# The first norm moved behind the first product, and gate biases and sinks loaded as one row

## Chip, core and metric

The kernel runs on one core of a Trainium2 chip. The metric is the device time of one execution in microseconds (us); lower is better. Engines are named as in the profile: PE is the matrix engine (PEld its weight loads), DVE the vector engine, ACT the scalar engine, POOL the GpSimd engine, SP the engine whose queue issues most DMAs.

## Reference

Two decoder layers of width 1024 over 256 tokens, float32. Only the start matters here: a norm of each token, then a product with `w_in`, whose column groups feed the mixers.

```python
def rmsnorm(x, g):
    xf = x.astype(jnp.float32)
    y = xf * lax.rsqrt(jnp.mean(xf * xf, axis=-1, keepdims=True) + EPS)
    return (y * g.astype(jnp.float32)).astype(x.dtype)
...
def mixer_block(h, w_in, conv_w, conv_b, b_igate, b_fgate, mlstm_norm_g, sinks,
                rel_bias, w_branch_m, w_branch_a, w_out):
    proj = h @ w_in
    mqk, mv, mo, mi, mf, aq, ak, av, ga, gb = jnp.split(proj, offsets, axis=-1)
...
for l in range(DEPTH):
    h = rmsnorm(x, norm_mix_g[l])
    x = x + mixer_block(h, w_in[l], conv_w[l], conv_b[l], b_igate[l], b_fgate[l], ...)
    h = rmsnorm(x, norm_mlp_g[l])
    x = x + sqrelu_mlp(h, w_up[l], w_down[l])
```

The norm of a token is one number per row, `r = rsqrt(mean(x*x) + EPS)`, so `(x * r * g) @ w` equals `r * ((x * g) @ w)`: the factor may be applied to the rows of the product.

## The kernel before

Tokens lie in two tiles of 128 (`tt` 0 and 1), the width of 1024 in eight blocks of 128 (`k` 0 to 7) and in two halves of 512 (`hf`). Every product is made in three passes: each operand is split into a rounded part (`hi`, `xh`) and the rest (`lo`, `xl`), and hi by hi, lo by hi and hi by lo are summed in PSUM (L220 to L222 with tokens as the stationary side, "xs"; L234 to L236 with weights as the stationary side, "ws").

Weights come in pieces of 128 x 1024 (512 KB). `pump_dma` (L114) issues the load of the next piece on SP into one of four buffers `raw`; `pump_hi` (L142) casts it to `hi` on ACT (L152); `pump_lo` (L123) subtracts on DVE (L127), which frees the raw buffer, and issues the next load. `hi` and `lo` have seven buffers each.

The order of all work is written by hand. `slots` is a list of steps, each 12 or 24 matmuls; `run_slots` (L191) emits for each slot first what is registered with `at`, then splits of pieces, then `at_late`, then `at_last`, then the matmuls of the slot, then what is registered with `after`. Each engine executes its own instructions in the order in which they were emitted, and waits where one needs a result of another engine. So an instruction that waits keeps back everything emitted later on its engine.

At the start, `setup_start` (L400) issues the loads of x (X, 128 x 2 x 1024) and of the first four pieces, then `small_loads` (L388): eleven small loads, of which six spread a few numbers to 128 partitions (`gb_bias`, `sink`). PE is kept busy with matmuls of a zero tile (`N_WARM`, L418, L424, L559).

`first_norm` (L524) squares X on ACT and DVE, takes the power -0.5 on POOL (`Norm.rstd`, L349), scales X by it (L532), transposes the 128 x 128 blocks on PE (L537) and multiplies by g while it splits into xh (ACT, L541) and xl (DVE, L547).

The first product, `mv` (columns 1024 to 2047 of `w_in`), has slots `s_mv` to `s_mv` + 7. Its first four slots take the two token tiles one after the other (head "t"): tile 0 on pieces 0 to 3, then tile 1 on them; the last four take piece by piece (tail "k"). `mv_evac` (L597) copies the four PSUM banks of it to `vm` behind slot `s_mv` + 7, two on ACT (L603) and two on DVE (L601). The next product, `kv` (four slots from `s_kv` = `s_mv` + 8, pieces 8 to 11), takes three of those banks again, so its first matmuls wait for these copies.

Beside `mv` run `setup_small` (L426, at slot `s_mv` + 2; masks and selectors on POOL) and `setup_cols` (L439, at slot `s_mv` + 4): two transposes on PE, the copies `cw` and `rbT` on DVE, then on POOL the table `Et` of the relative bias (a memset, 17 copies of a column of `rbT`, L450 and L455, and a DMA to DRAM, L457).

Of the kernel before, what the change touches and what calls it, by code (L numbers as in the profile page):

```python
# [17 lines left out]
P = 128  # L18
# [24 lines left out]
def trunk(ctx: ExitStack, tc: tile.TileContext, x, norm_mix_g, w_in, conv_w, conv_b, b_igate, b_fgate,  # L43
# [43 lines left out]
    def piece(w, kt, c0):  # L87
        def load(raw):
            nc.sync.dma_start(raw[:, :1024], w[kt * P : (kt + 1) * P, c0 : c0 + 1024])

        pieces.append((load, 1024))
        return len(pieces) - 1
# [21 lines left out]
    def pump_dma():  # L114
        j = n_dma[0]
        if j < len(pieces):
            raws[j] = wp.tile([P, 1040], F32, tag="raw", bufs=N_RAW, name=nm("raw"))
            pieces[j][0](raws[j])
            n_dma[0] += 1
# [3 lines left out]
    def pump_lo():  # L123
        for j in los:
            raw, n = raws.pop(j), pieces[j][1]
            hi, lo = pc[j]
            nc.vector.tensor_tensor(lo[:, :n], raw[:, :n], hi[:, :n].bitcast(F32), op=ALU.subtract)  # L127
            pump_dma()
        los.clear()

# [255 lines left out]
    N_WARM = (26, 16, 8)  # L386

    def small_loads():  # L388
        S0["b8"] = big8()
        rows = S0["rows"] = S0["b8"][:80, 0, 0:P]  # L390
        rb = S0["rb"] = const.tile([NB_BUCKETS, 16], F32, name="rb")
        nc.sync.dma_start(rb, rel_bias)
        for l in range(DEPTH):
            nc.sync.dma_start(gb_bias[:, l, 0:4], b_igate[l].partition_broadcast(P))
            nc.sync.dma_start(gb_bias[:, l, 4:8], b_fgate[l].partition_broadcast(P))
            nc.sync.dma_start(sink[:, l, :], attn_sinks[l].partition_broadcast(P))
            nc.sync.dma_start(rows[40 * l : 40 * l + 32, :], conv_w[l].rearrange("j (m c) -> (j m) c", c=P))
            nc.sync.dma_start(rows[40 * l + 32 : 40 * l + 40, :], conv_b[l].rearrange("(m c) -> m c", c=P))

    def setup_start():  # L400
        grow = big8()[:8, 0, 0:P]
        nc.sync.dma_start(X[:, 0, 0:512], xv[:, 0, 0:512])
        nc.sync.dma_start(X[:, 0, 512:], xv[:, 0, 512:])
        nc.sync.dma_start(grow, norm_mix_g[0].rearrange("(k c) -> k c", c=P))
        for i in range(N_RAW):
            if i == 3:
                nc.sync.dma_start(X[:, 1, :], xv[:, 1, :])
            pump_dma()
# [7 lines left out]
        pw = psA()  # L416
        for _ in range(N_WARM[0]):
            nc.tensor.matmul(pw[:, :P], mask, mask, start=True, stop=True)  # L418
        pg = psA()
        nc.tensor.transpose(pg[:, :8], grow, ident[:8, :8])  # L420
        S0["gcol"] = const.tile([P, KT], F32, name="gcol")
        S0["pg"], S0["pw"] = pg, pw
        for _ in range(N_WARM[1]):
            nc.tensor.matmul(pw[:, :P], mask, mask, start=True, stop=True)  # L424

    def setup_small():  # L426
        nc.vector.tensor_copy(identb, ident)
        nc.gpsimd.affine_select(
            out=mask, in_=mask, pattern=[[1, P]], compare_op=ALU.is_ge, fill=NEG, base=0, channel_multiplier=-1)
        nc.gpsimd.memset(vm[:, :, :, 256:257], 1.0)  # L430
        z = tmp()
        nc.gpsimd.memset(z, 0.0)
        nc.scalar.copy(Rs, z[:, 0:384])
        for r in (0, 32):
            nc.gpsimd.affine_select(out=z[r : r + 32, 0:4], in_=z[r : r + 32, 0:4], pattern=[[-1, 4]],
                                    compare_op=ALU.not_equal, fill=1.0, base=0, channel_multiplier=1)
        nc.scalar.copy(sel, z[:, 0:4])

    def setup_cols():  # L439
        pt = psB()  # L440
        nc.tensor.transpose(pt[:, :80], S0["rows"], ident[:80, :80])
        nc.vector.tensor_copy(cw, pt[:, :80])
        pt = psB()
        nc.tensor.transpose(pt[:16, :NB_BUCKETS], S0["rb"], ident[:NB_BUCKETS, :NB_BUCKETS])
        rbT = const.tile([16, NB_BUCKETS], F32, name="rbT")
        nc.vector.tensor_copy(rbT, pt[:16, :NB_BUCKETS])
# [77 lines left out]
    def first_norm(st, xtag, nxt):  # L524

        xh, xl = st["hT"] = xT_tiles(xtag)
        N = [Norm(0), Norm(1)]
        gcol, xn, pts = S0["gcol"], {}, {}

        def scale(tt, hf):  # L530
            xn[tt, hf] = tmp()
            nc.vector.tensor_scalar(xn[tt, hf], X[:, tt, hc(hf)], N[tt].r[:, :1], None, op0=ALU.mult)  # L532

        def tr(tt, hf):
            pts[tt, hf] = psB()
            for j in range(4):
                nc.tensor.transpose(pts[tt, hf][:, j * P : (j + 1) * P], xn[tt, hf][:, j * P : (j + 1) * P], ident)  # L537

        def hi(tt, ks):
            for k in ks:  # L540
                nc.scalar.activation(xh[:, k, tt * P : (tt + 1) * P], pts[tt, k // 4][:, k % 4 * P : (k % 4 + 1) * P],  # L541
                                     AF.Copy, scale=gcol[:, k : k + 1])

        def lo(tt, ks):
            for k in ks:
                s = slice(tt * P, (tt + 1) * P)
                nc.vector.scalar_tensor_tensor(xl[:, k, s], pts[tt, k // 4][:, k % 4 * P : (k % 4 + 1) * P],  # L547
                                               gcol[:, k : k + 1], xh[:, k, s].bitcast(F32), op0=ALU.mult,
                                               op1=ALU.subtract)

        N[0].square(0)
        N[0].square(1, "dve")
        N[0].rstd()
        nc.scalar.copy(gcol, S0["pg"][:, :8])
        pump_hi(0, 0)
        scale(0, 0)
        tr(0, 0)
        for _ in range(N_WARM[2]):
            nc.tensor.matmul(S0["pw"][:, :P], mask, mask, start=True, stop=True)  # L559
        pump_lo_part(0, 512)  # L560
        hi(0, (0, 1))
        lo(0, (0, 1))
# [3 lines left out]
        hi(0, (2, 3))  # L566
        pump_lo()
        lo(0, (2, 3))
        pump_hi(0, 2)
        N[1].square(0)  # L570
        N[1].square(1)
        pump_lo()
        N[1].rstd()
        scale(0, 1)
        pump_hi(0, 3)
        scale(1, 0)
        pump_lo()
        scale(1, 1)

        def tr_all(tt, hf):  # L580
            tr(tt, hf)
            hi(tt, range(4 * hf, 4 * hf + 4))
            lo(tt, range(4 * hf, 4 * hf + 4))

        for i in range(4):
            limits[nxt + i] = 3 + max(0, i - 1)
        slots[nxt + 1][0].insert(2, call(lambda: tr_all(1, 0)))
        slots[nxt + 2][0].insert(1, call(lambda: tr_all(0, 1)))
        slots[nxt + 2][0].insert(4, call(lambda: tr_all(1, 1)))


    def mixer(l, ta, tb):
        w = w_in[l]
        st = {}
        s_mv = xs_group(st, "mv", "hT", w, MV0, head="t")

        def mv_evac(tt, hf):  # L597
            o = vm[:, tt, 2 * hf : 2 * hf + 2, 0:256]
            i = st[("mv", tt, hf)].rearrange("p (h c) -> p h c", h=2)
            if hf:  # L600
# [145 lines left out]
        def cwc(j, m):  # L746
            return cw[:, 40 * l + j * 8 + m : 40 * l + j * 8 + m + 1]
# [318 lines left out]
    for l in range(DEPTH):  # L1066
# [9 lines left out]
        if l == 0:  # L1076
            at(s_mv + 2, setup_small)
# [84 lines left out]
```

## Time and profile before

| | us |
|---|---|
| median of 3 runs | 883.76 (883.75 to 883.88) |
| the profiled execution, its own time | 884.32 |
| its span in the profile | 882.5 |
| PE busy in the span | 868.5 (98%) |
| first matmul of the first product | at 9.21 |
| first matmul of kv | at 35.87 |
| last matmul | at 873.92 |

Times in the trace count from the start of the span; the 1.8 us between span and time lie around it. PE is busy almost throughout, so what counts is how late PE gets to a given matmul, and whether it is ever kept waiting after that. "Busy" of PE overstates in the first microseconds, since a matmul's end is modelled.

### The profile page before, as it was taken

The page shows a single profiled execution, that of the slowest core. Times are in us where ns is not written, and L with a number is a line of the kernel's source. Part 1 is how long each engine was busy: PE and PEld are TensorE (multiplying, and loading weights), DVE is VectorE, ACT ScalarE, POOL GpSimd, SP SyncE. Part 2 cuts the span into 40 slices and gives each one's busy share as a digit, 9 for nine tenths or more (in the row PEclk, how much of TensorE's full clock was granted, in tenths as well). Part 3 has the DMA queues.
Part 4 walks back from the last instruction along what each step waited for, and adds up shares of the span by engine and source line. Part 5 has one row for each costly group of instructions (what it writes and reads, how often), then busy time and mean ns, then how long its engine had stood idle before and what let it go on. Part 6 is the DMA issues. An engine that isn't in the chain of part 4 may idle for free.

```text
span 882.5 us, 15073 instructions
## 1 busy us (share of the span) xinstructions
PE 868.5 (98%) x5929; PEld 789.6 (89%) x5929; DVE 572.4 (65%) x928; ACT 468.2 (53%) x771; POOL 128.3 (15%) x164
## 2 busy tenths in 40 slices
PE   7999999999999999999999999999999999999996
PEld 5899889999989999998889997999998899999985
DVE  5758879666666654546574788876667764737363
ACT  5657776654355554544355557764634453636352
POOL 1360534120000000000002435322000000000000
PEclk9999999999999999999999999999999999999999
DMA  6875435445556747474655455354564466555621
GB/s 217 288 246 186 144 120 167 141 147 158 177 191 202 248 133 240 133 242 136 219 171 189 149 186 163 109 160 144 148 223 157 146 225 225 194 188 188 194 96 48
DMA packets 50711, 155.28 MB, mean 176 GB/s; under 512 B 7912, under 2 KB 10192, under 8 KB 50640
## 3 DMA queue, kind: packets, MB, share of 16 engines
q1 hardware_dynamic: 49456, 150.69, 52.8%
q0 software_dynamic: 896, 3.17, 1.0%
q8 instruction: 46, 0.75, 0.4%
q10 hardware_dynamic: 288, 0.46, 0.1%
q14 instruction: 25, 0.20, 0.1%
HBM read 153.23 MB, written 1.07 MB: 175 GB/s over the span
## 4 chain that ended last, share of the span: by engine, by line
PE 92%; DVE 3%; issue 2%; ACT 1%; POOL 1%; DMA 0%; POOLq 0%; SPq 0%; DVEq 0%; ACTq 0%
PE pa L220 13%; PE pa L221 13%; PE pa L222 12%; PE pa L235 10%; PE pa L234 10%; PE pa L236 10%; PE pb L235 5%; PE pb L234 5%; PE pb L236 5%; PE pb L859 1%; PE pb L322 1%; PE pb L879 1%; DVE lo L127 1%; PE pb L919 1%; PE pb L832 1%
## 5 line engine op out<-in xcount | busy, mean ns | idle before, releaser
L127 DVE TENSOR_TENSOR lo<-raw,hi 128x1024 fp32r<-128x1024 f32 (+1 forms) x276 | 332.0, 1226 | 137.5 <-ACT hi L152 134.4
L152 ACT CAST hi<-raw 128x1024 fp32r<-128x1024 f32 (+1 forms) x280 | 286.1, 1049 | 184.0 <-PE pa L222 48.1
L234 PE MATMUL pa<-xh,hi 128*128 128x256 f32 x864 | 246.4, 285 | 0.0
L235 PE MATMUL pa<-xl,hi 128*128 128x256 f32 x864 | 242.6, 281 | 0.0
L236 PE MATMUL pa<-xh,lo 128*128 128x256 f32 x864 | 241.7, 280 | 0.0
L234 PEld LDWEIGHTS pa<-xh,hi 128*128 128x128 f32 x864 | 162.7, 188 | 0.9 <-issue 0.3
L235 PEld LDWEIGHTS pa<-xl,hi 128*128 128x128 f32 x864 | 162.9, 189 | 0.3
L236 PEld LDWEIGHTS pa<-xh,lo 128*128 128x128 f32 x864 | 162.8, 188 | 0.0
L220 PE MATMUL pa<-hi,xh 128*128 128x512 f32 (+1 forms) x384 | 149.9, 390 | 1.8 <-ACT xh L541 1.8
L221 PE MATMUL pa<-lo,xh 128*128 128x512 f32 (+1 forms) x384 | 148.1, 386 | 0.5 <-DVE lo L127 0.4
L222 PE MATMUL pa<-hi,xl 128*128 128x512 f32 (+1 forms) x384 | 147.8, 385 | 0.0
L234 PE MATMUL pb<-xh,hi 128*128 128x256 f32 x384 | 107.6, 280 | 0.0
L235 PE MATMUL pb<-xl,hi 128*128 128x256 f32 x384 | 107.6, 280 | 0.0
L236 PE MATMUL pb<-xh,lo 128*128 128x256 f32 x384 | 107.3, 280 | 0.0
L220 PEld LDWEIGHTS pa<-hi,xh 128*128 128x128 f32 x384 | 72.2, 188 | 15.4 <-ACT xh L541 2.0
L222 PEld LDWEIGHTS pa<-hi,xl 128*128 128x128 f32 x384 | 72.1, 188 | 15.4
L221 PEld LDWEIGHTS pa<-lo,xh 128*128 128x128 f32 x384 | 72.2, 188 | 15.2 <-DVE lo L127 1.6
L349 POOL TENSOR_TENSOR sm<-sm,mhalf 128x1 f32<-128x1 f32 x9 | 6.6, 731 | 500.0 <-DVE sm L348 500.0
L235 PEld LDWEIGHTS pb<-xl,hi 128*128 128x128 f32 x384 | 72.3, 188 | 1.8
L234 PEld LDWEIGHTS pb<-xh,hi 128*128 128x128 f32 x384 | 72.2, 188 | 1.7
L236 PEld LDWEIGHTS pb<-xh,lo 128*128 128x128 f32 x384 | 72.3, 188 | 0.0
L220 PE MATMUL pa<-hi,b 128*128 128x512 f32 x124 | 48.8, 394 | 0.0
(210 smaller groups left out, 986.1 us busy)
## 6 DMA issues: line engine op xcount, KB each, us to landing
raw<-in_w_in SPq DMA_DIRECT2D x104, 512.0 KB, 4.5
raw<-in_w_up SPq DMA_DIRECT2D x64, 512.0 KB, 4.7
raw<-in_w_down SPq DMA_DIRECT2D x64, 512.0 KB, 4.3
raw<-in_w_branch_a SPq DMA_DIRECT2D x16, 512.0 KB, 3.5
raw<-in_w_branch_m SPq DMA_DIRECT2D x16, 512.0 KB, 4.1
raw<-in_w_out SPq DMA_DIRECT2D x16, 512.0 KB, 4.5
b<-ed SPq DMA_DIRECT2D x4, 512.0 KB, 5.2
g<-in_mlstm_norm_g POOLq DMA_DIRECT2D x2, 512.0 KB, 5.8
```

The source lines that it names most:

```text
L127: nc.vector.tensor_tensor(lo[:, :n], raw[:, :n], hi[:, :n].bitcast(F32), op=ALU.subtract)
L152: nc.scalar.copy(hi[:, :n], raw[:, :n])
L220: nc.tensor.matmul(b, xh[:, kt, s], wh[:, c], start=first, stop=False)
L221: nc.tensor.matmul(b, xh[:, kt, s], wl[:, c], start=False, stop=False)
L222: nc.tensor.matmul(b, xl[:, kt, s], wh[:, c], start=False, stop=last)
L234: nc.tensor.matmul(o, wh[:, c], xh[:, kt, :], start=first and half == 0, stop=False, skip_group_check=True)
L235: nc.tensor.matmul(o, wh[:, c], xl[:, kt, :], start=False, stop=False, skip_group_check=True)
L236: nc.tensor.matmul(o, wl[:, c], xh[:, kt, :], start=False, stop=last, skip_group_check=True)
L322: nc.tensor.transpose(pt[:, j * P : (j + 1) * P], src[:, j * P : (j + 1) * P], ident)
L832: nc.tensor.matmul(sp[:, P : 3 * P], q[:, P:T], kh[:, gk, :], start=False, stop=False, skip_group_check=True)
L859: nc.tensor.transpose(tp[:, j * P : (j + 1) * P], L[:, j * P : (j + 1) * P], ident)
L879: nc.tensor.matmul(o, va[:, 0, vs], PT[:, 0:T], start=(h0 % 4 == 0), stop=False, skip_group_check=True)
```

## The change

Four things change, all at the start of the first layer.

1. The first product takes x times g, without the norm. `first_norm` transposes X itself (L554), multiplies by g on DVE for a half tile at once into a float32 buffer `xg` (L560), and splits that (ACT L564, DVE L567) into `uh`, `ul`. The second halves of X follow inside slots `s_mv` + 2 and + 3 (`rest`). The squares and `rstd` of the two tiles (`norm`) come at the end of the preparations of slots `s_mv` + 3 and + 4. `mv_evac` multiplies by `r` of the token.
2. The other products of the layer still take the normed input. `rows` (at slot `s_mv` + 6) turns `r` into a row over tokens on all partitions with two matmuls (L613) and an ACT copy (L616); `normed` multiplies `xg` by it on DVE for four blocks at once (L621) and splits again (ACT L323, DVE L324), the first half at slot `s_mv` + 6, the second at + 7.
3. `mv` goes piece by piece from the start (head "k"), and piece 0 is loaded and split in two halves.
4. The small loads are six: both layers' convolution rows in two, and gate biases and sinks as one row of 48 numbers, which `setup_cols` spreads with a matmul (L459) and two DVE copies. `norm_mix_g` is loaded from ACT's queue. `setup_small` moves from slot `s_mv` + 2 to + 6, its two ACT copies to + 9.

```diff
+    def pump_hi_part(a, b):
+        j = n_split[0] - (1 if a else 0)
...
+        nc.scalar.copy(pc[j][0][:, a:b], raws[j][:, a:b])
...
-        for l in range(DEPTH):
-            nc.sync.dma_start(gb_bias[:, l, 0:4], b_igate[l].partition_broadcast(P))
-            nc.sync.dma_start(gb_bias[:, l, 4:8], b_fgate[l].partition_broadcast(P))
-            nc.sync.dma_start(sink[:, l, :], attn_sinks[l].partition_broadcast(P))
...
+        nc.sync.dma_start(rows[0:64, :], conv_w.rearrange("l j (m c) -> (l j m) c", c=P))
+        nc.sync.dma_start(rows[64:80, :], conv_b.rearrange("l (m c) -> (l m) c", c=P))
+        row = S0["row"] = S0["b8"][0:1, 0, 512:560]
...
+        nc.scalar.dma_start(grow, norm_mix_g[0].rearrange("(k c) -> k c", c=P))
+        for tt in range(2):
+            nc.sync.dma_start(X[:, tt, 0:512], xv[:, tt, 0:512])
+        pump_dma(2)
+        pump_dma()
+        pump_dma()
+        for tt in range(2):
+            nc.sync.dma_start(X[:, tt, 512:], xv[:, tt, 512:])
+        pump_dma()
         small_loads()
...
     def setup_cols():
...
+        nc.tensor.matmul(pt[:, :48], ones[0:1, 0:1].to_broadcast([1, P]), S0["row"], start=True, stop=True)
+        nc.vector.tensor_copy(gb_bias, pt[:, 0:16].rearrange("p (l c) -> p l c", l=DEPTH))
+        nc.vector.tensor_copy(sink, pt[:, 16:48].rearrange("p (l h) -> p l h", l=DEPTH))
...
+        def times_g(tt, hf):
+            nc.vector.tensor_tensor(xg[sl(tt, hf)], pts[tt, hf].rearrange("p (k t) -> p k t", k=4),
+                                    gcol[:, 4 * hf : 4 * hf + 4].unsqueeze(2).to_broadcast([P, 4, P]), op=ALU.mult)
...
+        def rest(tt):
+            tr(tt, 1)
+            times_g(tt, 1)
+            hi(tt, 1)
+            lo(tt, 1)
+
+        def norm(tt):
+            N[tt].square(0)
+            N[tt].square(1)
+            N[tt].rstd()
...
+        for tt in range(2):
+            slots[nxt + 2 + tt][0].insert(1, call(lambda tt=tt: rest(tt)))
+            at_last(nxt + 3 + tt, lambda tt=tt: norm(tt))
...
+        def rows():
+            pr = psB()
+            for tt in range(2):
+                nc.tensor.matmul(pr[:, tt * P : (tt + 1) * P], N[tt].r[:, 0:1].to_broadcast([P, P]), ident, start=True,
+                                 stop=True, skip_group_check=True)
+            S0["R"] = tmp()
+            nc.scalar.copy(S0["R"][:, 0:T], pr[:, 0:T])
+            st["hT"] = xT_tiles(xtag)
+
+        def normed(c):
+            s = (slice(None), slice(4 * c, 4 * c + 4), slice(None))
+            nc.vector.tensor_tensor(xg[s], xg[s], S0["R"][:, 0:T].unsqueeze(1).to_broadcast([P, 4, T]), op=ALU.mult)
+            evac_split(xg[s], st["hT"][0][s], st["hT"][1][s])
+
+        at(nxt + 6, rows)
+        at(nxt + 6, lambda: normed(0))
+        at(nxt + 7, lambda: normed(1))
...
-        s_mv = xs_group(st, "mv", "hT", w, MV0, head="t")
+        s_mv = xs_group(st, "mv", "hT" if l else "hU", w, MV0, head="t" if l else "k")
...
+            if l == 0:
+                r = S0["r"][tt]()
+                if hf:
+                    nc.vector.tensor_scalar(o, i, r, None, op0=ALU.mult)
+                else:
+                    nc.scalar.activation(o, i, AF.Copy, scale=r)
...
-            at(s_mv + 2, setup_small)
+            at(s_mv + 6, setup_small)
+            at(s_mv + 9, setup_copies)
             at(s_mv + 4, setup_cols)
```

Where this puts the instructions shows in three places. First POOL, at the powers of the norm: `sm<-sm,mhalf` is `rstd` of a token tile, `b<-rbT` are copies of the table, `ed` is its DMA to DRAM. Before:

```order
L349 TENSOR_TENSOR sm_174<-sm_173,mhalf 128x1
L349 TENSOR_TENSOR sm_225<-sm_224,mhalf 128x1
L428 AFFINE_SELECT mask<-mask 128x128
L430 MEMSET vm 128x8
L432 MEMSET tmp_286 128x512
L435 AFFINE_SELECT tmp_286<-tmp_286 32x4 x2
L448 MEMSET b_6_97 16x384
L450 COPY b_6_97<-rbT 16x16
L455 COPY b_6_97<-rbT 16x3
```

Now, from the last copies of the table on (the first tile's power stands ahead of the table's memset, as L359):

```order
L472 COPY b_6_99<-rbT 16x10 x2
L472 COPY b_6_99<-rbT 16x12
L472 COPY b_6_99<-rbT 16x14
L472 COPY b_6_99<-rbT 16x15
L474 DMA ed<-b_6_99 16x384
L359 TENSOR_TENSOR sm_358<-sm_357,mhalf 128x1
L436 AFFINE_SELECT mask<-mask 128x128
L438 MEMSET vm 128x8
```

The power of token tile 1 stood ahead of the whole table and now stands behind it.

Second PE, between the sixth and the seventh piece of the first product (`pa` are its banks; `pb<-ident,sm` are the two matmuls of `rows`). Before, at the end of the sixth piece (`hi_341`) and the start of the seventh:

```order
L220 MATMUL pa_243<-hi_341,xh_165 128x512
L221 MATMUL pa_243<-lo_342,xh_165 128x512
L222 MATMUL pa_243<-hi_341,xl_166 128x512
L220 MATMUL pa_240<-hi_389,xh_165 128x512
L221 MATMUL pa_240<-lo_390,xh_165 128x512
```

Now, at the end of the sixth (`hi_241`) and the start of the seventh:

```order
L230 MATMUL pa_201<-hi_241,xh_139 128x512
L231 MATMUL pa_201<-lo_242,xh_139 128x512
L232 MATMUL pa_201<-hi_241,xl_140 128x512
L613 MATMUL pb_406<-ident,sm_291 128x128
L613 MATMUL pb_406<-ident,sm_358 128x128
L230 MATMUL pa_198<-hi_244,xh_139 128x512
```

The two matmuls that need both powers stand in PE's order with 24 matmuls of the first product behind them.

Third DVE, from the copies of `setup_cols` to the evacuation of the first product (`lo<-raw,hi` is a piece's subtraction, `vm<-pa` the evacuation, `b_11` is `xg`, `tmp_409` the row of `r`). Before:

```order
L446 COPY rbT<-pb_363 16x32
L127 TENSOR_TENSOR lo_390<-raw_222,hi_389 128x1024
L127 TENSOR_TENSOR lo_393<-raw_236,hi_392 128x1024
L127 TENSOR_TENSOR lo_396<-raw_300,hi_395 128x1040
L127 TENSOR_TENSOR lo_422<-raw_345,hi_421 128x1040
L127 TENSOR_TENSOR lo_440<-raw_399,hi_439 128x1040
L127 TENSOR_TENSOR lo_458<-raw_403,hi_457 128x1040
L601 COPY vm<-pa_241 128x2x256
```

Now:

```order
L463 COPY rbT<-pb_317 16x32
L129 TENSOR_TENSOR lo_348<-raw_248,hi_347 128x1040
L358 TENSOR_SCALAR sm_357<-sm_143 128x1
L129 TENSOR_TENSOR lo_374<-raw_252,hi_373 128x1040
L435 CAST identb<-ident 128x128
L621 TENSOR_TENSOR b_11_141<-b_11_141,tmp_409 128x1024
L324 TENSOR_TENSOR xl_412<-b_11_141,xh_411 128x1024
L129 TENSOR_TENSOR lo_417<-raw_256,hi_416 128x1040
L621 TENSOR_TENSOR b_11_141<-b_11_141,tmp_409 128x1024
L324 TENSOR_TENSOR xl_412<-b_11_141,xh_411 128x1024
L129 TENSOR_TENSOR lo_438<-raw_283,hi_437 128x1040
L640 TENSOR_SCALAR vm<-pa_199,sm_291 128x2x256
```

The four wide instructions of `normed` now stand between the pieces' subtractions and ahead of the evacuation; on ACT the two casts of `normed` (L323) stand likewise ahead of its part of the evacuation (L642), each with the cast of a kv piece behind it.

More of the change, by code (lines that the diff above doesn't have):

```diff
@@ L384, in trunk @@
     S0 = {}
[L386 removed]
+    N_WARM = (22, 6, 14)
     def small_loads():
@@ L536, in tr @@
             for j in range(4):
[L537 to L559, printed above, removed]
+                c = hf * 512 + j * P
+                nc.tensor.transpose(pts[tt, hf][:, j * P : (j + 1) * P], X[:, tt, c : c + P], ident)
+        def sl(tt, hf):
+            return (slice(None), slice(4 * hf, 4 * hf + 4), slice(tt * P, (tt + 1) * P))
```

112 lines of the change are left out of this document (57 added, 55 removed).

## Prediction

> **What bounds the kernel now.** First the head of the page and its chain of waits (part 4): PE is busy 98% of the span, and 92% of the chain that ends last is PE.
>
> ```profile
> span 882.5 us, 15073 instructions
> PE 92%; DVE 3%; issue 2%; ACT 1%; POOL 1%; DMA 0%; POOLq 0%; SPq 0%; DVEq 0%; ACTq 0%
> ```
>
> Then busy time by stretches (first the stretch and its length, then PE's busy time in it).
>
> ```profile
> 36.00:60.00 24.00, 23.98 (x202) 23.77 (x201) 14.22 (x19) 12.15 (x16) 9.84 (x9) 1.00 0.75 241
> 60.00:100.00 40.00, 39.43 (x335) 38.46 (x335) 30.27 (x71) 27.99 (x55) 13.09 (x23) 1.00 0.60 199
> 100.00:200.00 100.00, 100.00 (x734) 91.03 (x734) 76.77 (x187) 65.27 (x147) 31.85 (x29) 1.00 0.47 144
> 200.00:400.00 200.00, 199.97 (x1345) 183.36 (x1345) 122.03 (x131) 95.21 (x115) 2.05 (x3) 1.00 0.58 192
> 400.00:600.00 200.00, 199.79 (x1351) 179.16 (x1350) 139.14 (x267) 115.91 (x220) 49.87 (x58) 1.00 0.52 163
> 600.00:872.00 272.00, 271.97 (x1791) 247.79 (x1790) 164.07 (x207) 127.76 (x172) 9.97 (x9) 1.00 0.52 171
> ```
>
> From 36 to 872 us PE is idle 0.86 us in all (0.02+0.57+0+0.03+0.21+0.03). So whatever shifts the start of kv, the second product, shifts the end by as much, and at most those 0.9 us of waits could swallow a delay. The change is over when kv has started. The timeline of PE gives the marks, the first product and kv's three banks:
>
> ```profile
> 9.21 0.50 PE L220 MATMUL pa<-hi,xh 128*128 128x512 f32 x1 [1.79 <-ACT xh L541]
> ...
> 35.63 0.40 PE L222 MATMUL pa<-hi,xl 128*128 128x512 f32 x1
> 35.87 0.28 PE L234 MATMUL pa<-xh,hi 128*128 128x256 f32 x1
> ...
> 37.12 0.39 PE L220 MATMUL pa<-hi,xh 128*128 128x264 f32 x1
> ```
>
> The first product starts at 9.21 and kv at 35.87. Its 96 matmuls follow each other every 0.23 us (35.63 to 35.87), 22.1 us; the other 4.6 are waits and small matmuls between. The question is when kv starts in the changed kernel.
>
> **What comes earlier.** Half of piece 0 is cast by itself, and no norm stands ahead. A DVE instruction that waited for X and SP's issues of small loads show when transfers land:
>
> ```profile
> 4.09 0.69 DVE L344 CUSTOM_DVE_ANT_0 tmp<-X 128x512 f32<-128x512 f32 x1 [3.10 <-DMA X<-in_x]
> ...
> 7.84 0.33 SPq L396 DMA_DIRECT2D sink<-in_attn_sinks  x1
> 9.13 0.33 SPq L397 DMA_DIRECT2D b<-in_conv_w  x1
> 10.49 0.29 SPq L398 DMA_DIRECT2D b<-in_conv_b  x1
> 11.76 0.35 SPq L394 DMA_DIRECT2D gb_bias<-in_b_igate  x1
> 13.02 0.35 SPq L395 DMA_DIRECT2D gb_bias<-in_b_fgate  x1
> 14.81 2.17 SPq L89 DMA_DIRECT2D raw<-in_w_in  x4
> ```
>
> X's first tile is there at 4.1. Each of SP's issues is kept back by the DMA eight places earlier, so they date the landing of pieces 0, 1, 2, of X's second tile and of piece 3: one 512 KB transfer per 1.3 us. Now the first half of piece 0 lands between 5.9 (half way from 4.1 to 7.84, as its bytes are) and 7.84; with a cast the first matmul comes at 6.6 to 8.4, I take 7.8: 1.4 us earlier. Pieces 4 to 7 are issued from 11.8 instead of 14.81, since fewer small ones stand before them. None of this reaches kv, as the next part shows. The new head order needs a piece per 12 matmuls, 2.8 us, against 1.3 us per landing; short waits there cost nothing for the same reason.
>
> **What stands on the path to kv.** I follow it back from kv. Its first matmul takes over a bank that ACT must evacuate (L642); ahead of that on ACT stand both casts of `normed` and those of two kv pieces; `normed` needs the row of `r`, made by two PE matmuls (L613), which need tile 1's power on POOL; POOL makes that behind the whole bias table; the table needs `rbT` from DVE; and ahead of `rbT` on DVE stands X times g of the last quarter, behind piece 6's subtraction and the first tile's squares. These rows (groups by line and shape) price it:
>
> ```profile
> raw<-in_w_in SPq DMA_DIRECT2D x104, 512.0 KB, 4.5
> ...
> L127 DVE TENSOR_TENSOR lo<-raw,hi 128x1024 fp32r<-128x1024 f32 x268 | 322.1, 1225 | 131.3 <-ACT hi L152 128.3 <-PE pa L236 1.7 <-PE pa L222 0.2
> L314 DVE TENSOR_TENSOR xl<-pb,xh 128x512 fp32r<-128x512 f32 x32 | 22.1, 691 | 29.9 <-ACT xh L313 29.8
> L348 DVE TENSOR_SCALAR sm<-sm 128x1 f32<-128x1 f32 x9 | 1.9, 213 | 2.7 <-ACT tmp L342 2.6
> L442 DVE COPY cw<-pb 128x80 f32<-128x80 f32 x1 | 0.2, 238 | 0.0
> L446 DVE COPY rbT<-pb 16x32 f32<-16x32 f32 x1 | 0.2, 168 | 0.0
> ...
> L152 ACT CAST hi<-raw 128x1024 fp32r<-128x1024 f32 x272 | 277.6, 1048 | 175.5 <-PE pa L222 48.1 <-PE pb L235 31.1 <-DMA raw<-in_w_in 25.6
> L342 ACT ACTIVATE tmp<-X 128x512 f32<-128x512 f32 x17 | 10.7, 632 | 23.6 <-DVE X L1088 12.6 <-DVE X L474 9.8 <-DMA X<-in_x 1.2
> L313 ACT CAST b<-tmp 128x512 fp32r<-128x512 f32 x16 | 8.7, 619 | 0.0
> L342 ACT ACTIVATION_READ_ACCUMULATOR tmp<-X 128x1 f32 x17 | 3.2, 188 | 0.0
> L603 ACT COPY vm<-pa 128x512 f32<-128x512 f32 x4 | 2.2, 588 | 3.1 <-PE pa L222 3.1
> ```
>
> Step 1, to piece 6. The same bytes stand ahead of X's last part as before, so it lands at 11.8 and frees the issue of piece 4; piece 5 waits for the landing of piece 3 (13.0), piece 6 goes out at 13.4. At 4.5 us from issue to landing and 1.3 between, they land at 16.3, 17.6, 18.9; in an empty queue it may be up to 0.8 less. I take 18.4 for piece 6.
>
> Step 2, to `rbT`. Piece 6: cast 1.05, subtraction 1.22, so 20.7. X times g for tile 0's second half 0.69 (as L314), its cast 0.62, piece 7's cast 1.05, two squares with their reads 1.64, DVE's sum 0.21, X times g for tile 1 0.69, cast 0.62, subtraction 0.69: 26.9. PE, which needs these last two for slot 4, waits there some 3 us. Then four small copies 0.75 (0.24 and three of 0.17): `rbT` at 27.6; before, POOL had it at 26.25.
>
> Step 3, POOL. The timeline of before:
>
> ```profile
> 26.25 2.16 POOL L450 COPY b<-rbT 16x16 f32<-16x16 f32 x1 [7.51 <-DVE rbT L446]
> 28.37 4.13 POOL L455 COPY b<-rbT 16x3 f32<-16x3 f32 x16
> 32.80 0.71 POOL L457 DMA_DIRECT2D ed<-b  x1 [0.30 <-POOL b L455]
> 33.51 0.58 POOL L366 DMA_DIRECT2D g<-in_mlstm_norm_g  x1
> ...
> 26.02 3.51 DVE L127 TENSOR_TENSOR lo<-raw,hi 128x1024 fp32r<-128x1024 f32 x3
> ...
> L455 POOL COPY b<-rbT 16x10 f32<-16x10 f32 x2 | 0.3, 182 | 0.0
> L349 POOL TENSOR_TENSOR sm<-sm,mhalf 128x1 f32<-128x1 f32 x9 | 6.6, 731 | 500.0 <-DVE sm L348 500.0
> ```
>
> The 17 copies took 6.25 us, though one alone takes 0.18: the first, of 2.16, ends where DVE's second subtraction ends. In the new order two subtractions stand beside them, not three or more, so I take 17 x 0.18 = 3.06 plus 2 x 1.22: 5.5, between 3.1 (no overlap) and 6.25 (as it was). The Trainium skill (SBUF — State Buffer, Who interferes with whom) states that a DVE instruction with two SBUF inputs and a GpSimd instruction that reads SBUF keep each other out for a whole instruction; that agrees with 2.16 beside 0.18, gives the 5.5, and by the bare row of 6.25 the sum would be 0.75 longer. With 0.30 and 0.71 for the DMA and 0.73 for the power: 34.8. PE, done with slot 5 at about 30.6 (26.9, then 0.9 for four matmuls of slot 4 and 2.8 for slot 5), waits 4.2 us for it.
>
> Step 4, to the evacuation. Two matmuls and the copy of the row 0.8; multiply 1.22; cast 1.05; subtraction 1.22; the kv piece's subtraction 1.22, which stands ahead of the second multiply on DVE; multiply 1.22; cast 1.05; a kv piece's cast 1.05; evacuation 0.59: 9.4 us, so kv starts at 44.2. PE has 24 matmuls for this time, 5.5 us, and waits the other 3.9.
>
> The end: 44.2 - 35.87 = 8.3 us later. The second tile of kv also waits for DVE's evacuation, as before (37.12), a little longer now: 0.1. The profiled execution took 884.32 us (span 882.5); the median is 0.56 below it, and I put the shift on the median: 883.76 + 8.4 = 892.2. Fewer transposes and matmuls of zeros on PE lie ahead of these waits and are worth nothing. The moved `setup_small` stands on POOL behind the power, its two ACT copies behind the evacuation: nothing on the path.
>
> **The rivals.**
> *Faster:* the waits do not arise, and only the earlier start counts. Leaving 2.9 of the 4.6 us of small matmuls and short waits, PE would need 7.8 + 22.1 + 2.9: kv at 32.8, 3.1 us earlier, 880.7. It decides at one point: step 4 would have to fit into PE's own 5.5 us, and the table would have to be done before 27.3. Against it: step 4's nine instructions follow one another, each needs the one ahead or stands behind it. Chance 0.03.
> *Only step 4 counts:* the table is ready when PE is. Then kv starts at 30.6 + 9.4 = 40.0: 4.1 later, 887.9. It needs `rbT` by 23.4, that is piece 6 some 4 us sooner. Chance 0.06. Were PE never late at all, it would reach `rows` at 27.3 and kv would start at 36.7, 884.6: within 0.2%. Chance 0.03.
> *The clock falls in the wait:* beyond the delay, matmuls after it run slowly. The tail of before shows such a fall (the eighth number is the granted clock):
>
> ```profile
> 874.00:875.00 1.00, 0.20 (x2) 0.00 (x0) 0.87 (x2) 0.10 (x1) 0.00 (x0) 1.00 0.12 45
> 878.00:879.00 1.00, 0.00 (x0) 0.00 (x0) 0.65 (x2) 0.45 (x1) 0.00 (x0) 0.86 0.00 0
> 879.00:880.00 1.00, 0.00 (x0) 0.00 (x0) 0.00 (x0) 0.00 (x0) 0.00 (x0) 0.50 0.68 253
> ```
>
> PE's last work ends at 874.2, and the clock is halved from about 878.7: after 4.5 us of rest. The two waits are 4.2 and 3.9 us, just below. If it falls in the second and takes as long to come back as it took to fall, 4.5 us at half speed cost 2.2 us: 894.4. In the first it costs nothing, since step 4 hides it. The Trainium skill (TensorE: Matmul & The Clock Gate, The HAM clock gate) has the clock halved after an idle window of about 3.4 us, whose phase runs free; by that rule a wait of 3.9 us may or may not cover one. Chance 0.13.
>
> **How the numbers follow.** Forecast 892.2, chance 0.72. Its own bounds: piece 6 earlier by 0.3 and POOL by 2.4 gives 889.5; piece 6 later by 0.5 and POOL by 0.75 gives 893.5. A further 0.03 is for a part I have not seen. The range of 888.8 to 894.8 takes in the forecast's bounds and most of the clock's case, and leaves out the first two rivals. About 0.2% (1.8 us) is what a measurement of this kernel tells from no change. Faster 0.03, same 0.03, slower 0.94.
>
> **What would show it.** In the changed profile: first product at 7 to 8.4; a wait of PE at L230 in its fifth piece for ACT's cast L564; at L613 of 3 to 5 us for POOL L359, which starts right behind L474; at L244 of about 4 us for ACT L642; kv from 42 to 45; no idle PE of note behind that. I am wrong if L613 does not wait, if kv starts before 40, or if later waits shrink by more than 0.9 us.

## The result and the profile after

The changed kernel takes 893.69 us (median of 4 runs, 893.01 to 894.23), the kernel before 883.76: ratio 1.0112, 95% interval 1.0099 to 1.0124. It is 9.9 us slower. The profiled execution took 894.06 us.

The head of the page and its chain (parts 1 and 4): PE carries 89% of the chain instead of 92%, the weights' transfers have 2% instead of 0 (DMA), ACT 2% instead of 1%, and "issue" (time in which the engine waited for nothing that the profile shows) 3% instead of 2%. These shares say where the path runs, not what the loss is: 2% of 892 is 18 us, more than the whole loss, since for most of the first 20 us the path now follows the landing of the weights while PE works beside it.

```profile
span 892.3 us, 15055 instructions
...
PE 89%; DVE 3%; issue 3%; ACT 2%; DMA 2%; POOL 1%; SPq 0%; POOLq 0%; DVEq 0%; ACTq 0%
```

From 47 us on, PE is idle 0.85 us in 834, as it was before from 36 us on (a row by stretch; the second number is the stretch, the third PE's busy time). The loss is therefore nearly all ahead of that point.

```profile
47.00:881.00 834.00, 833.15 (x5727) 762.58 (x5727) 542.85 (x872) 440.94 (x721) 116.69 (x130) 1.00 0.54 173
```

The timeline of PE has the marks: the first product begins at 6.98 (before: 9.21), the second (kv, the keys' and gates' product) at 43.44 (before: 35.87). Two waits stand between that the kernel before did not have in this place, and a third, of 0.8, at the row of `r`.

```profile
6.98 0.48 PE L230 MATMUL pa<-hi,xh 128*128 128x512 f32 x1
...
20.47 0.19 PE L457 MATMUL pb<-ident,rb 32*16 32x32 f32 x1
22.57 0.42 PE L459 MATMUL pb<-b,ones 1*128 1x48 f32 x2 [1.90 <-DVE b L560]
23.21 0.65 PE L230 MATMUL pa<-hi,xh 128*128 128x512 f32 x1 [0.23 <-ACT xh L564]
...
32.71 0.38 PE L613 MATMUL pb<-ident,sm 128*128 128x128 f32 x2
33.92 0.49 PE L613 MATMUL pb<-ident,sm 128*128 128x128 f32 x2 [0.82 <-POOL sm L359]
...
39.56 0.40 PE L232 MATMUL pa<-hi,xl 128*128 128x512 f32 x1
43.44 0.39 PE L244 MATMUL pa<-xh,hi 128*128 128x256 f32 x1 [3.48 <-ACT vm L642]
...
43.90 0.41 PE L244 MATMUL pa<-xh,hi 128*128 128x256 f32 x1
...
47.13 0.37 PE L230 MATMUL pa<-hi,xh 128*128 128x264 f32 x1
```

Read the matmul at 23.21: its shape takes 0.39 us elsewhere, here 0.65. The windows say why (the eighth number is the granted clock, as a mean over the window): it was near half in both stretches that follow the long waits.

```profile
23.00:30.00 7.00, 5.91 (x13) 3.96 (x14) 5.14 (x11) 6.11 (x13) 2.77 (x10) 0.53 0.70 198
43.00:47.00 4.00, 3.56 (x18) 3.56 (x19) 4.00 (x6) 4.00 (x7) 0.00 (x0) 0.61 0.43 114
```

POOL shows the table, its store and the power of tile 1 behind them:

```profile
28.14 1.04 POOL L467 COPY b<-rbT 16x16 f32<-16x16 f32 x1 [1.55 <-DVE rbT L463]
29.14 3.11 POOL L472 COPY b<-rbT 16x3 f32<-16x3 f32 x16
32.56 0.71 POOL L474 DMA_DIRECT2D ed<-b  x1 [0.30 <-POOL b L472]
33.29 0.58 POOL L359 TENSOR_TENSOR sm<-sm,mhalf 128x1 f32<-128x1 f32 x1
```

The sixteen copies at L472 one by one (shortest, median and longest in ns, then the first and last start):

```profile
L472 POOL COPY b<-rbT x16: 177/182/1194, 29.1 to 32.1; 16x3 f32<-16x3 f32 x3, 16x4 f32<-16x4 f32 x2, 16x6 f32<-16x6 f32 x2, 16x10 f32<-16x10 f32 x2
```

To split the 9.8 us of span (882.5 to 892.3) one more mark is needed, the last of the 48 transposes of layer 0's attention heads. Its row, after:

```profile
L903 PE MATMUL pb<-ident,L x48: 270/272/329, 95.3 to 170.7; 128*128 128x128 f32 x48
```

and before:

```profile
L859 PE MATMUL pb<-ident,L x48: 270/272/328, 86.3 to 161.5; 128*128 128x128 f32 x48
```

Start of kv: 43.44 - 35.87 = 7.6 later. From there to the last of these transposes: 127.3 instead of 125.6, 1.6 more. From there to the end: 721.6 instead of 721.0, 0.6 more. Of the 1.6, 1.4 are the second slow stretch: from 43.90 to 47.13 there are 15 matmuls of 256 and 264 columns, 0.215 us each, where at the full clock they follow each other every 0.12: 3.23 us instead of 1.80.

### The profile page after: what moved, and what is told of

Read it like the earlier page. It is cut to its first block, busy times and chain, and to the rows that moved or that the text cites. A ratio compares the mean times of both kernels' runs of the same rounds, so it can differ in the third digit from the quotient of the medians.

```text
span 892.3 us, 15055 instructions
## 1 busy us (share of the span) xinstructions
PE 873.7 (98%) x5927; PEld 795.4 (89%) x5927; DVE 575.8 (65%) x921; ACT 469.2 (53%) x764; POOL 127.0 (14%) x165
## 4 chain that ended last, share of the span: by engine, by line
PE 89%; DVE 3%; issue 3%; ACT 2%; DMA 2%; POOL 1%; SPq 0%; POOLq 0%; DVEq 0%; ACTq 0%
PE pa L230 11%; PE pa L244 11%; PE pa L245 11%; PE pa L232 11%; PE pa L231 11%; PE pa L246 11%; PE pb L245 5%; PE pb L244 5%; PE pb L246 5%; DMA raw<-in_w_in 2%; PE pb L903 1%; PE pb L923 1%; PE pb L332 1%; PE pb L963 1%; DVE lo L129 1%
## 5 line engine op out<-in xcount | busy, mean ns | idle before, releaser
L162 ACT CAST hi<-raw 128x1024 fp32r<-128x1024 f32 (+1 forms) x279 | 284.9, 1048 | 180.9 <-PE pa L232 43.9
L230 PE MATMUL pa<-hi,xh 128*128 128x512 f32 (+1 forms) x384 | 151.4, 394 | 1.1 <-ACT xh L564 1.1
L230 PEld LDWEIGHTS pa<-hi,xh 128*128 128x128 f32 x384 | 73.1, 190 | 14.7 <-ACT xh L564 2.0
L359 POOL TENSOR_TENSOR sm<-sm,mhalf 128x1 f32<-128x1 f32 x9 | 6.4, 715 | 512.6 <-DVE sm L358 512.6
L230 PE MATMUL pa<-hi,b 128*128 128x512 f32 x124 | 49.1, 396 | 0.0
```

The source lines that it names most:

```text
L162: nc.scalar.copy(hi[:, :n], raw[:, :n])
L230: nc.tensor.matmul(b, xh[:, kt, s], wh[:, c], start=first, stop=False)
```

## The experiments

Theory A: the loss is one chain that stands ahead of kv (POOL's power of tile 1, the row of `r`, the normed X, the first product's evacuation), and the clock's fall behind PE's waits comes on top. The rivals are named in each expectation. Ratios are to the kernel before, measured beside each run (its median there 883.7 to 884.3).

**1. The row alone.** Before, with only the loads and the spreading product of the change:

```
 (before)
-        for l in range(DEPTH):
-            nc.sync.dma_start(gb_bias[:, l, 0:4], b_igate[l].partition_broadcast(P))
...
+        nc.sync.dma_start(row[:, 16:48], attn_sinks.rearrange("(o l) h -> o (l h)", o=1))
...
+        nc.tensor.matmul(pt[:, :48], ones[0:1, 0:1].to_broadcast([1, P]), S0["row"], start=True, stop=True)
```

> The kernel before with one part of the change alone: gate biases and sinks as one row spread by a product, and one load each for the convolution's weights. Theory A (the loss lies in the first product's new order: the row of r, the product's scaling by it and the evacuation stand ahead of the next product): no loss from this part, 883.3 to 884.6, the first matmul of the keys' product at 35.9 give or take 0.4. Rival C (the small loads are the cost: the row's matmul and its evacuation, or the table behind them, hold PE): 886 or more, and PE waits at the row's matmul or later than before at the keys' product.

884.09 us, ratio 1.0002 (0.9993 to 1.0011). The start of kv:

```profile
36.15 0.28 PE L234 MATMUL pa<-xh,hi 128*128 128x256 f32 x1
```

By itself this part costs nothing and gains nothing; rival C falls.

**2. The norm's part alone.** The change with the loads, the columns and the table of before:

```
 (after)
+            nc.sync.dma_start(gb_bias[:, l, 0:4], b_igate[l].partition_broadcast(P))
...
-        nc.tensor.matmul(pt[:, :48], ones[0:1, 0:1].to_broadcast([1, P]), S0["row"], start=True, stop=True)
```

> The changed kernel with the small loads, the columns and their table as they were before, so the norm's part of the change alone. Theory A: the loss stays or grows, 893 to 899, because the ten broadcast loads stand in SP's queue ahead of pieces 4 to 7, which then land later (keys' product from 43.4 to 48). Rival C (small loads are the cost): within 1 us of 883.8.

896.85 us, ratio 1.0154 (1.0134 to 1.0173). The waits of PE:

```profile
PE pa L230 <- ACT xh L559: 6.4, 2, 5.6
PE pa L244 <- ACT vm L637: 3.5, 1, 3.5
```

The whole loss is in the norm's part, and the row softens it by 3.2 us: without it PE's wait at the fifth piece is 5.6 us long instead of some 2. The same loads were worth nothing in the old order (run 1). In that order PE's longest waits are for the norm (1.8 us for ACT's xh at L541 and 1.1 us for DVE's scaling at L532), and those for a piece's remainder add up to 0.4 us.

**3. Other banks for kv.**

```
-        at(s_kv, lambda: st.update({("kv", 0): psA(), ("kv", 1): psA(), "kk": psA()}))
+        at(s_kv, lambda: st.update({("kv", 0): psB(), ("kv", 1): psB(), "kk": psB()}))
```

> The changed kernel, but the keys' product takes its three PSUM banks from the other four, which are free by then, so that it needs no evacuation of the first product. Theory A (after the product's own matmuls end at 39.96, PE waits 3.5 us for that evacuation, and the clock falls in this wait, which costs some 1.5 us of slow matmuls): the wait and the slow stretch go, the keys' product starts at 40.0 to 40.4, time 893.7 - 3.5 - 1.5 = 888.7 (888.0 to 889.5). Rival D (the halves of the normed X come as late as the banks): the wait moves to the cast of the normed X, and the time stays within 1 us of 893.7. Rival E (the clock's fall is not due to this wait): 890.2, with slow matmuls still at the start of the keys' product.

889.04 us, ratio 1.0056 (1.0041 to 1.0071): 4.7 us less than the change. The timeline of PE, where the kv product follows the last matmul of the first one:

```profile
39.51 0.39 PE L232 MATMUL pa<-hi,xl 128*128 128x512 f32 x1
39.74 0.28 PE L244 MATMUL pb<-xh,hi 128*128 128x256 f32 x1
```

As theory A has it: the wait of 3.5 us and the slow stretch behind it are both gone, and no other wait takes their place. From kv's start to the last transposes of the heads it takes 126.0 us, 1.3 less than in the change, which prices the slow stretch a second time:

```profile
L903 PE MATMUL pb<-ident,L x48: 270/272/329, 90.3 to 165.7; 128*128 128x128 f32 x48
```

**4. The table later.**

```
-            at(s_mv + 4, setup_cols)
+            at(s_mv + 5, setup_cols)
```

> The changed kernel with the columns and their table one slot later, so that on POOL the power of tile 1 stands ahead of the 17 copies and the store. As the prediction had it (PE waits 4.2 us at the row of r for POOL): 893.7 - 4.2 = 889.5. Theory A (the trace of the change shows 0.8 us of wait there, PE itself being late because of its wait at the fifth piece and of slow matmuls behind that): no wait at the row of r, keys' product at 42.2 to 42.7, time 892.5 to 893.1; the same slow matmuls from 23 to 30. Rival F (with no wait left there, PE waits as much longer at the next place): same as the change, 893.7.

894.65 us, ratio 1.0118 (1.0097 to 1.0139), but its four runs lie between 891.86 and 896.55, further apart than those of any other kernel here; the profiled one is the fastest. Its PE timeline:

```profile
22.56 0.51 PE L230 MATMUL pa<-hi,xh 128*128 128x512 f32 x1 [3.02 <-ACT xh L564]
...
31.43 0.61 PE L613 MATMUL pb<-ident,sm 128*128 128x128 f32 x4
...
41.10 0.39 PE L244 MATMUL pa<-xh,hi 128*128 128x256 f32 x1 [3.50 <-ACT vm L642]
```

No wait at the row of `r`, as all expected, but theory A's numbers miss both ways: kv starts at 41.1, not 42.2 to 42.7, because in this execution the clock did not fall at the fifth piece though the wait there was 3.0 us; and the median gains nothing. The table's place is worth no gain by itself. Rival F's time lies inside the spread, but its mechanism is not in the profile: the wait ahead of kv is 3.50 us, as in the change (3.48), and not longer. The longer runs had the slower clock: the recorded mean granted clocks are 0.995, 0.992, 0.989 and 0.988 at 891.86, 893.95, 895.36 and 896.55 us. Where in those runs the clock fell is not shown, since only the fastest was profiled.

**5. PE kept busy in the last wait.**

```
+        def keep_busy():
+            pk = psB()
+            for _ in range(30):
+                nc.tensor.matmul(pk[:, :P], identb, identb, start=True, stop=True)
+        if l == 0:
+            at(s_kv, keep_busy)
```

> The changed kernel with 30 small matmuls (128 columns, of an identity with itself, their result unused) put in PE's wait of 3.5 us ahead of the keys' product, nothing else. Theory A (the slow matmuls behind that wait are the clock's answer to an idle PE and cost some 1.5 us beside the wait itself): keys' product still at 43.2 to 43.8, its first matmuls 0.12 us apart and not 0.21, time 892.2 (891.6 to 892.8). Rival G (the fall has another cause, or costs nothing at the end): same as the change, 893.7, matmuls 0.21 us apart as before.

893.10 us (892.26 to 895.42), ratio 1.0113 (1.0096 to 1.0130). By the time, inconclusive: the expected 1.5 us are less than the spread of its four runs. The profile agrees with theory A: the granted clock behind kv's start (42.34) is full.

```profile
42.00:47.00 5.00, 4.47 (x35) 4.26 (x36) 5.00 (x6) 4.40 (x8) 0.00 (x0) 1.00 0.47 123
```

One execution does not show the mechanism, though: the clock did not fall at the fifth piece either, which nothing in the edit brings about, and in run 10 below it stays full behind a wait of 2.2 us that nothing fills. PE was at the row of `r` the sooner, and only waited longer there, 2.1 us instead of 0.8; kv follows 9.5 us behind, as in the change:

```profile
32.82 0.49 PE L613 MATMUL pb<-ident,sm 128*128 128x128 f32 x2 [2.10 <-POOL sm L359]
...
42.34 0.39 PE L244 MATMUL pa<-xh,hi 128*128 128x256 f32 x1 [1.80 <-ACT vm L642]
```

**6. The second halves of X earlier**, and piece 3's split behind them:

```
-        limits[nxt + 1] = 3
+        limits[nxt + 1] = 2
+        limits[nxt + 2] = 3
         for tt in range(2):
-            slots[nxt + 2 + tt][0].insert(1, call(lambda tt=tt: rest(tt)))
+            slots[nxt + 1 + tt][0].insert(1, call(lambda tt=tt: rest(tt)))
```

> The changed kernel with the second halves of X one slot earlier and piece 3 split behind them, so that PE's fifth piece needs no longer wait for tile 0's second half; the table stays ahead of tile 1's power on POOL. Theory A (the delays stand in one chain: whoever makes PE early gives it the wait that the prediction named): the wait of 1.9 us ahead of the fifth piece and the slow matmuls behind it go, PE reaches the row of r before 29 and waits there 3 to 4.5 us for the power behind the table, keys' product at 40.0 to 41.5, time 890 to 892. Rival H (PE's late fifth piece is itself the loss): no such wait at the row of r, keys' product at 38.5 or earlier, 888.5 or less.

888.35 us, ratio 1.0051 (1.0036 to 1.0066). The row of `r` and the start of kv (this kernel's lines are one higher there):

```profile
26.30 0.38 PE L614 MATMUL pb<-ident,sm 128*128 128x128 f32 x2
29.89 0.49 PE L614 MATMUL pb<-ident,sm 128*128 128x128 f32 x2 [3.21 <-POOL sm L359]
...
39.40 0.38 PE L244 MATMUL pa<-xh,hi 128*128 128x256 f32 x1 [1.90 <-ACT vm L643]
```

Theory A's mechanism shows (PE on time, and then 3.2 us of wait for the power behind the table, the wait that the prediction named), but its time was too high by 1.7: kv started 0.6 sooner than the lower end, and behind the heads the same matmuls took less time (below). Rival H's condition, no such wait, does not hold either; its time does, by another way. The clock is near half behind both waits here:

```profile
30.00:34.00 4.00, 4.00 (x12) 3.21 (x13) 2.02 (x2) 2.24 (x3) 2.57 (x7) 0.57 0.44 139
39.00:45.00 6.00, 5.41 (x31) 5.20 (x32) 5.93 (x7) 4.78 (x8) 0.00 (x0) 0.72 0.50 141
```

From the row of `r` to kv it is 9.5 us here too (29.89 to 39.40), as in the change (33.92 to 43.44), though PE ran at half the clock for part of it.

Kv starts 4.0 us sooner than in the change, but the span is 5.8 us shorter (886.5). The difference lies behind the heads. First the change's last matmul, then this run's transposes of layer 0's heads and its last matmul:

```profile
883.46 0.28 PE L232 MATMUL pb<-hi,b 128*128 128x256 f32 x1
```

```profile
L904 PE MATMUL pb<-ident,L x48: 270/273/329, 91.8 to 167.1; 128*128 128x128 f32 x48
...
877.71 0.28 PE L232 MATMUL pb<-hi,b 128*128 128x256 f32 x1
```

From the last of these transposes to the last matmul it takes 712.8 us in the change (170.7 to 883.46) and in runs 2, 3, 4, 5 and 7, 712.4 in the kernel before (161.5 to 873.92), 712.5 in run 1, but 710.6 or 710.7 in runs 6, 8, 9 and 10, the four that have this run's edit. No wait and no fall of the clock makes the difference; it is spread over the whole stretch. Why the matmuls follow each other a little faster there was not found.

**7. Banks and table together** (the edits of runs 3 and 4).

> The changed kernel with both earlier edits: the keys' product in the other four banks, and the columns and table behind tile 1's power. Theory A: no wait at the row of r and none ahead of the keys' product; what is left is the wait ahead of the fifth piece and its slow matmuls: keys' product at 37.4 with a full clock (885.3), 40.0 where the clock falls in that wait (888.5); by the run, 885 to 889. Rival D (the halves of the normed X hold PE next): a wait at the keys' product for the cast or the remainder of the normed X, 889 or more.

889.97 us (887.73 to 891.75), ratio 1.0067 (1.0050 to 1.0085), 1 us above the range. Kv starts inside its bounds, with the slow clock behind the fifth piece, but a wait appears far behind, at the transposes of an early attention head:

```profile
38.26 0.28 PE L244 MATMUL pb<-xh,hi 128*128 128x256 f32 x1
```

```profile
PE pa L230 <- ACT xh L564: 3.4, 2, 2.7
PE pb L903 <- POOL L L896: 1.1, 1, 1.1
```

So rival D is not the reason; that wait of 1.1 us was in nobody's theory. Behind it the clock fell once more: from 91 to 95 us the mean granted clock is 0.57. From kv's start to the last transposes of the heads (166.7) it takes 128.4 us, 2.4 more than in run 3, which is why this run is no faster than run 3 though its kv starts 1.5 us sooner.

**8. All edits together**, with squares, row of `r` and normed X one slot earlier as well:

```
-            at_last(nxt + 3 + tt, lambda tt=tt: norm(tt))
+            at_last(nxt + 2 + tt, lambda tt=tt: norm(tt))
...
-        at(nxt + 6, rows)
-        at(nxt + 6, lambda: normed(0))
-        at(nxt + 7, lambda: normed(1))
+        at(nxt + 5, rows)
+        at(nxt + 5, lambda: normed(0))
+        at(nxt + 6, lambda: normed(1))
...
-            at(s_mv + 4, setup_cols)
+            at(s_mv + 6, setup_cols)
```

> The changed kernel with all that the runs named put right: second halves of X one slot earlier, the squares of X one slot earlier, the row of r and the first half of the normed X one slot earlier, the second half one slot earlier too, the table behind them on POOL, the keys' product in the other four banks. Theory A (the change's early first matmul is worth its 2.5 us once the chain behind it is out of PE's way): keys' product at 33.0 to 34.0, 2 to 3 us before the kernel before, no slow matmuls, time 881.4 (880.8 to 882.5). Rival J (what the early start gains is lost to the weights' landing, which no order of work changes): keys' product at 35.5 or later, 883.5 or more.

880.71 us, ratio 0.9966 (0.9953 to 0.9979): 3.1 us faster than the kernel before and 13 faster than the change. The timeline of PE:

```profile
24.87 0.49 PE L614 MATMUL pb<-ident,sm 128*128 128x128 f32 x2 [1.57 <-POOL sm L359]
...
33.91 0.39 PE L232 MATMUL pa<-hi,xl 128*128 128x512 f32 x1
34.14 0.28 PE L244 MATMUL pb<-xh,hi 128*128 128x256 f32 x1
```

Kv starts 1.7 us before that of the kernel before and waits for nothing; rival J falls. Theory A's kv (33.0 to 34.0) and time (880.8 to 882.5) are both missed by 0.1. The wait of 1.1 us at the heads is in this kernel too. Its marks:

```profile
L904 PE MATMUL pb<-ident,L x48: 270/272/328, 85.4 to 160.7; 128*128 128x128 f32 x48
...
871.40 0.28 PE L232 MATMUL pb<-hi,b 128*128 128x256 f32 x1
```

So of kv's lead of 1.7 us 0.8 is left at the last transposes (160.7 instead of 161.5). Another 1.7 us is gained behind them, by the faster matmuls of run 6 (710.7 us instead of 712.4). By its profiles, then, about two thirds of this kernel's lead at the last matmul (2.5 us) have nothing to do with the early start.

**9. The table one slot sooner in the combined kernel** (`s_mv + 5`).

> The combined kernel (all edits together) with the columns and the table one slot sooner, still behind tile 1's power on POOL, so that the sums of the table's columns do not wait on DVE behind the normed X. Theory A (in the two kernels with the table moved back, PE waits 1.1 us at the transposes of an early attention head for POOL, which it does not in the others; the late table pushes the bias's copies on ACT into that stretch): the wait of 1.1 us there goes, 879.6 (879.0 to 880.5). Rival L (the 1.1 us there are not the table's): the wait stays, 880.7.

882.51 us, ratio 0.9978 (0.9967 to 0.9988). The wait at the heads did not go, it grew:

```profile
PE pb L904 <- POOL L L897: 1.5, 1, 1.5
```

Behind it the clock fell (0.57 in the window). Kv started still earlier than in run 8, and the lead was lost at the heads:

```profile
32.32 0.28 PE L244 MATMUL pb<-xh,hi 128*128 128x256 f32 x1
...
85.00:89.00 4.00, 3.42 (x17) 3.26 (x17) 2.83 (x10) 3.64 (x12) 3.07 (x3) 0.57 0.12 46
...
L904 PE MATMUL pb<-ident,L x48: 270/273/475, 84.8 to 161.5; 128*128 128x128 f32 x48
```

Kv starts 3.6 us before that of the kernel before, but the last transposes come at 161.5 in both: nothing of the lead is left. What this run gains on the kernel before, it gains behind the heads, as run 6 does.

Theory A is wrong on this wait. Rival L is right that it stays, but not on the time. The wait shows in the three kernels that have both kv in the other banks and the table moved back (7, 8, 9), and in none that has one of the two only (3, 4, 10). Why the two together bring it was not found.

**10. The combined kernel in the old banks.**

> The combined kernel without the bank edit: the keys' product takes over the first product's banks, as in the change. Theory A (the evacuation of the first product can only begin when its last matmul is done, at 33.9 to 34.2, and stands on ACT behind casts): PE waits for the evacuation again, at least 1.2 us and up to 5, keys' product at 35.4 to 39, time 882 to 886. Rival M (with the normed X made early enough the evacuation is quick, and the banks are not needed): wait under 0.7 us, 880.7 to 881.4.

884.50 us, ratio 1.0003 (0.9994 to 1.0012).

```profile
24.20 0.49 PE L614 MATMUL pb<-ident,sm 128*128 128x128 f32 x2 [0.73 <-POOL sm L359]
35.87 0.39 PE L244 MATMUL pa<-xh,hi 128*128 128x256 f32 x1 [2.20 <-ACT vm L643]
```

As theory A has it: PE waits 2.2 us for the evacuation, and kv starts at 35.87, as in the kernel before. ACT shows why the evacuation is late: it stands behind the second cast of the normed X and two casts of kv pieces.

```profile
32.27 1.05 ACT L323 CAST xh<-b 128x1024 fp32r<-128x1024 f32 x1 [3.17 <-DVE b L622]
33.22 2.01 ACT L162 CAST hi<-raw 128x1040 fp32r<-128x1040 f32 x2
35.14 1.26 ACT L643 ACTIVATE vm<-pa,sm 128x512 f32<-128x512 f32 x2
```

In the kernel before kv takes over the same banks without a wait at its start. So the banks alone do not cost the lead; the banks together with these casts ahead of the evacuation do. The other way out, the evacuation ahead of the casts, was not tried. That the medians agree too is partly chance: the profiled execution, this kernel's fastest (883.37 at a mean clock of 0.998), ends its matmuls 1.1 us sooner than the kernel before by the faster stretch behind the heads, while the other nine lie at 884.4 to 885.0 with a mean clock of 0.995.

## Why the prediction was right

The forecast was 892.2, the result 893.69: inside the range, by the chain that it named, though 0.2 above the forecast's own bounds (889.5 to 893.5). That it came so near is in part luck: kv started 0.8 us sooner than forecast, and behind kv came 1.4 us of slow matmuls and 0.6 us of a longer rest that the forecast did not have. What took place is the forecast's chain together with the rival that the clock falls. Point by point:

- *A shift of kv is a shift of the end.* It held for the change: 0.85 us of idle PE behind kv, 0.86 before. It missed that the same matmuls took 0.6 us longer from the heads' transposes to the end. It is no rule for a kv that starts earlier: in run 9 a lead of 3.6 us was lost at the heads.
- *The early first product does not reach kv.* First matmul at 6.98 (forecast 7.8, range 6.6 to 8.4). It held: in the change the chain is far longer than this lead, and in run 10, with the chain shortened, the evacuation behind the casts still takes it back.
- *Steps 1 and 2, to `rbT`.* Piece 6's cast began at 19.6, 1.2 after the forecast of its landing (18.4). From there to the end of `rbT` it took 8.4 us, not the 9.2 of the sum, so `rbT` was done at 28.0 (27.6). Two misses nearly cancelled. The wait ahead of the fifth piece, "some 3 us", is there: 2.1 at L459 and L230, and then 0.9. L459, which is first in PE's order, was not named, but it waits for the same X times g.
- *Step 3, POOL.* **This term was mis-sized:** the table took 4.1 us (28.14 to 32.25), not 5.5. The two collisions with DVE's subtractions both came: the first copy took 1.04, and one of the other sixteen 1.19. Wrong was the undisturbed copy. One takes 0.18, but POOL starts the next before it ends: they follow each other about every 0.13 us, so the fifteen others took 2.0 us, not 2.7. The power ended at 33.9, not 34.8.
- *The wait at the row of `r`, 4.2 us.* **This term was mis-sized too:** it measured 0.8. POOL was 0.9 sooner, and PE came 2.1 later than forecast (32.7, not 30.6), mostly since it ran the fifth piece at half the clock: its last 18 matmuls before the row, from 26.89 on, took 5.8 us, where 0.23 each makes 4.1. It changed the sum little, because kv depends on the power and not on PE's arrival. Run 6, where PE is on time, shows the named wait: 3.2.
- *Step 4, 9.4 us from the row to kv.* It measured 9.5, in the change and in run 6. Kv at 43.4 (forecast 44.2); PE's wait 3.5 (3.9). Run 3 shows which link counts: without the evacuation at its end the wait is gone.
- *The clock.* The rival "the clock falls in the wait" had 0.13 and took place, twice. The step that failed is the measure: the 4.5 us of rest in the tail of before was taken for the length of wait that it takes. Waits of 1.9 plus 0.2 and of 3.5 us sufficed. The first fall came behind the wait at the fifth piece, which the rival left out, and was hidden: where it did not come (run 5), PE just waited longer for POOL. The second cost 1.4 us, where 2.2 had been worked out. With it the sum is 7.6 + 1.4 + 0.2 + 0.6 = 9.8.

## What to carry to other kernels

A factor that moves from a product's operand to its evacuation also moves the computation of that factor onto the evacuation's path: follow what must be done before the banks come free, engine by engine, before counting the early start as gained. Where the next product takes over those banks and the evacuation stands behind other work on its engine, the early start is given back (run 10: kv no earlier than in the kernel before); other banks take that wait away (runs 8 and 10 differ in the banks alone, 880.7 and 884.5). Then look for the next place that gives the lead back: in run 8 half of it, in run 9 all of it was gone by the heads. Price every new wait of PE, those of 1 to 2 us too, with the slow matmuls that may follow it. And compare the same stretch in both kernels before putting a gain down to its cause: here some 2 us came from matmuls far behind the change.

## What the runs showed of the hardware

- The clock's fall does not have a fixed threshold here. It fell after 1.9 us of wait with a few small products around it (the change), and again after 1.9 us (run 6, at 39.40), and at the heads, where PE has only short work between its waits, after 1.1 us (run 7) and 1.5 us (run 9). It did not fall after 3.0 (run 4, at 22.56), 2.1 (run 5, at 32.82) or 2.2 (run 10, at 35.87), nor after the 1.1 us at the heads in run 8. The Trainium skill (TensorE: Matmul & The Clock Gate, The HAM clock gate) tells of a free-running window of about 3.4 us in which PE must be idle; the free phase agrees with these traces, a full 3.4 us of idleness as the condition does not, and the measurement decides.
- Slow stretches lasted 3.3 us (43.9 to 47.2) or 6.9 (23.2 to 30.1) in the change, near one and two such windows by the same section.
- The granted clock varies from one execution of the change to the next, and the time with it: 893.01, 893.33, 894.06 and 894.23 us at mean clocks of 0.995, 0.993, 0.991 and 0.990. The kernel before has no such wait in its middle: its four runs measured beside these lay within 0.13 us, though beside run 1 they spread from 883.05 to 884.34.
- Short copies on POOL overlap: each takes 0.18 us, and sixteen of them, one of which was held up to 1.19, started from 29.1 to 32.1 in the change.
- The same matmuls can take a few tenths of a per cent more or less time without a wait or a fall of the clock: 712.4, 712.8 and 710.6 us from the last transposes of layer 0's heads to the last matmul, alike in all profiles of a group of kernels.
